# Attention outputs of a two-layer transformer block: V as the moving operand of its products instead of the stationary one

## The chip, the core and the metric

The kernel runs on one core of one Trainium2 chip. A core has five engines with queues of their own: TensorE (PE in the views, its weight loads PEld), VectorE (DVE), ScalarE (ACT), GpSimd (POOL) and SyncE (SP), which issues the transfers. TensorE reads both operands from SBUF: the stationary one (`lhsT`) is loaded first, then the moving one (`rhs`) streams through; results land in PSUM, from where VectorE or ScalarE fetch them. The metric is device time in microseconds of the whole program.

## What is computed

Two layers work on 512 latent tokens and 256 context tokens of width 1024. Each layer has attention with three groups of heads of 64 columns, then an output projection and a SwiGLU. Cut to what matters here:

```python
# A: 6 heads, 2 kv heads; keys: 512 latent + 256 context
oa = weigh(softmax(scores(qa, ka_all)), va_all)
# B: 4 heads, differential, then an RMS norm over the 64 columns of a head
p  = softmax(scores(q1, k1_all)) - lam * softmax(scores(q2, k2_all))
ob = rmsnorm(weigh(p, vb_all), g_subln) * (1 - lam_init)
# C: 6 heads, 2 kv heads; a band of up to 3 blocks of 128 keys + 256 context keys + a sink logit
p  = softmax(concat([s_loc, scores(q, kc), sink]))
oc = weigh(p_loc, v_blk) + weigh(p_ctx, vc)
ox = merge_heads(concat([oa, ob, oc]))      # then x + gate * (ox @ w_out)
```

In layer 0 the context tokens are queries as well (against context keys alone); in layer 1 only latent tokens are.

## The kernel before

All work is recorded as operations, and a planner (`Plan`) then puts them in an order by list scheduling, with a price for each (`Plan.price`) and with a choice between engines where an operation names two (`act_dve`, `dve_pool`, `plan.any`). The order of issue of each engine is fixed from then on; since all instructions are issued in one place, every row of the profile has the line 377. The sequence of the units of attention is written out in `ORDER` (letters A, B, C; small letters are steps of the modulation, P0 to P2 the projections).

A unit of A covers two heads (one of each kv head) and 256 queries as two tiles of 128; a unit of B two heads and 256 queries; a unit of C six heads and 128 queries. Layer 0 has 9 units of A, 6 of B and 6 of C, layer 1 has 6, 4 and 4. Scores are made with queries in partitions, in a PSUM tile `S` (two of them); VectorE finds the maximum of a row, ScalarE writes the exponentials to `P` and their sum to `rsum`. In A and C, `scale_rows` then multiplies P by the inverse of that sum, in place. In B, P1 - lambda P2 is formed unnormalised, and the sum goes into the later norm.

For the product with V, P is transposed on TensorE, 128 x 128 at a time, four (C: three) into one PSUM tile `T` (four of them), which is copied to an SBUF tile `pt`. In `pv_pair` the block of V (128 keys x 64 columns) is the stationary operand and `pt` (256 queries, in C 384) the moving one; the two heads of a pair write partitions 0 to 63 and 64 to 127 of `acc`, in f32. So the output comes with head columns in partitions, as the output projection wants it, and a copy to `o` ends units of A and C. `PV_RUN` puts the products of two key blocks together. In B the squares of `acc` are summed over partitions by a product with `hsel` (128 stationary columns, 2 moving ones), the inverse root is spread over partitions by a copy `rb` and a product with the identity, fetched as `rsb`, and multiplied in together with `gsub`.

The planner prices a product in f32 by the columns of its moving operand, with half the price where the output has 64 partitions:

```python
            share = {32: 4, 64: 2}.get(out.shape[0], 1)
            return max(n * 4 / 2400, 0.107) / share + 0.003
```

Of the kernel before, what the change touches and what calls it, by code (L numbers as in the profile page):

```python
# [34 lines left out]
FF_ADA = "dddd"  # L35
PV_RUN = {"A": 2, "B": 2, "C": 2}
QK_AHEAD = 238
# [12 lines left out]
SB = 32.0 ** -0.5  # L50
SLOTS = {"u": 39, "pt": 8, "s": 7, "y": 24, "rb": 2, "S": 2, "T": 4, "ropeG": 1}

# [328 lines left out]
def dit_block(  # L381
# [13 lines left out]

    pools = {tag: ctx.enter_context(tc.tile_pool(name="p" + tag, bufs=SLOTS[tag])) for tag in ("u", "pt", "s", "y", "rb")}
    cp = ctx.enter_context(tc.tile_pool(name="cp", bufs=1))
# [10 lines left out]
    def new(tag, shape, name, dt=F32):  # L408
        return plan.tile(pools[tag], [128] + list(shape), dt, tag, nm(name))
# [16 lines left out]
    def C(shape, name, dt=F32):  # L426
        return cp.tile([128] + list(shape), dt, tag=name, name=name)
# [247 lines left out]
    for l in range(2):  # L675
# [93 lines left out]
        else:  # L769
# [10 lines left out]
            act.copy(maskR, mst)  # L780
            hsel = C([2], "hsel")
            dve.memset(hsel, 0.0)
            for h in range(2):
                dve.memset(hsel[64 * h:64 * h + 64, h:h + 1], 1.0)
            ropeA = C([NX, 2, 64], "ropeA")
# [223 lines left out]

        def scale_rows(P, s):  # L1010

            plan.any([("dve", "tensor_scalar_mul", (P, P, s), {}),
                      ("act", "activation", (P, P, AF.Identity), {"scale": s})])

        def spread(rps, o, rr, n):

            rb = new("rb", [6, 64], "rb")
            dve_pool.tensor_copy(rb[:, 0:2 * n], rr.rearrange("p (h o) -> p h o", o=1).to_broadcast([128, 2 * n, 64]))
            for j in range(n):
                pe.matmul(rps[:, o + 128 * j:o + 128 * j + 128],  # L1020
                          lhsT=rb[:, 2 * j:2 * j + 2].rearrange("p h d -> p (h d)"), rhs=ident, start=True, stop=True)

        def pv_pair(acc, Ps, off, heads, kbs):

            kbs = list(kbs)
            for n0, run in pv_runs(kbs, PV_RUN["B" if heads[0] in (2, 4) else "A"]):
                pts = []
                for n in run:
                    t = PT()
                    with plan.together():  # L1030
                        for h in range(2):
                            for i in range(2):
                                pe.transpose(t[:, 256 * h + 128 * i:256 * h + 128 * i + 128],
                                             Ps[h][i][:, off + 128 * n:off + 128 * n + 128], ident)
                    pt = new("pt", [2, 256], "pt")
                    act_dve.copy(pt, t.rearrange("p (h n) -> p h n", h=2))
                    pts.append(pt)
                with plan.together():
                    for n, pt in zip(run, pts):
                        for h in range(2):  # L1040
                            pe.matmul(acc[64 * h:64 * h + 64, 0:256], lhsT=v_block(heads[h], kbs[n]), rhs=pt[:, h, :],
                                      start=(n == 0), stop=(n == len(kbs) - 1))

        def pv_runs(kbs, size):

            m = -(-len(kbs) // size)
            cuts = [len(kbs) * k // m for k in range(m + 1)]
            return [(a, range(a, b)) for a, b in zip(cuts, cuts[1:])]

# [38 lines left out]
        def attn_a():  # L1088
            stk = stack_ac("a")
            yield  # L1090
            Kx, Kc = stk[2:]
            for p, r, i0 in units(range(3)):
                k0 = 0 if r == 0 else 512
                Ps, rsum = ([], []), tiny(4)
                for j in range(2):
                    prods = []
                    for g in range(2):
                        q = q_block(stk, p, g, r, i0 + j)
                        prods.append([(q, Kx[hl][:, g], Kc[:, 2 * hl + g]) for hl in range(2)])
                    pair = score_pair(r, prods, [rsum[:, 2 * j + g:2 * j + g + 1] for g in range(2)])  # L1100
                    rr = inverse(rsum[:, 2 * j:2 * j + 2], 2)
                    for g in range(2):
                        scale_rows(pair[g][:, k0:768], rr[:, g:g + 1])
                        Ps[g].append(pair[g])
                acc = PT()
                pv_pair(acc, Ps, k0, (0, 1), range(k0 // 128, 6))
                act_dve.copy(o_cols(p, 1, r, 128 * i0, 256)[:, 0], acc[:, 0:256])
                yield

        def attn_b():  # L1110
            for p, r, i0 in units(range(2)):
# [4 lines left out]
                k0 = 0 if r == 0 else 512  # L1116
                Ps, rsum = ([], []), tiny(4)
                for j in range(2):
# [9 lines left out]
                    for hh, (P1, P2) in enumerate(pairs):  # L1128
                        dve.scalar_tensor_tensor(P1[:, k0:768], P2[:, k0:768], cf[:, hh:hh + 1], P1[:, k0:768],
                                                 op0=ALU.mult, op1=ALU.add)  # L1130
                        Ps[hh].append(P1)
                acc = PT()
                pv_pair(acc, Ps, k0, (2 + 2 * p, 3 + 2 * p), range(k0 // 128, 6))

                sq = S2([256], "sqb")
                act.activation(sq, acc[:, 0:256], AF.Square)
                for j in range(2):
                    pe.matmul(acc[:, 256 + 2 * j:258 + 2 * j], lhsT=sq[:, 128 * j:128 * j + 128], rhs=hsel, start=True, stop=True)
                w = tiny(4)
                dve.scalar_tensor_tensor(w, rsum, EPS, rsum, op0=ALU.mult, op1=ALU.mult)  # L1140
                ms = tiny(4)
                dve.scalar_tensor_tensor(ms, acc[:, 256:260], 1.0 / 64, w, op0=ALU.mult, op1=ALU.add)
                rs = tiny(4)
                pool.tensor_tensor(rs, ms, mhalf[:, 0:4], ALU.pow)
                spread(acc, 256, rs, 2)
                rsb = S2([256], "rsb")
                act_dve.copy(rsb, acc[:, 256:512])
                dve.scalar_tensor_tensor(o_cols(3 + p, 1, r, 128 * i0, 256)[:, 0], acc[:, 0:256], gsub[:, l:l + 1], rsb,
                                         op0=ALU.mult, op1=ALU.mult)
                yield  # L1150

        def attn_c():
# [4 lines left out]
            for r, i in ctx_first:  # L1157
# [3 lines left out]
                nk = 256 + nl  # L1161
                Ps, n2, rsum = ([], []), tiny(6), tiny(6)
                for j in range(3):
# [25 lines left out]
                    for g in range(2):  # L1189
                        P = new("u", [640], "P")  # L1190
                        c1 = slice(2 * j + g, 2 * j + g + 1)
                        act.activation(P[:, 0:nk], ss[g][:, 0:nk], AF.Exp, bias=n2[:, c1], accum_out=rsum[:, c1])
                        Ps[g].append(P)
                e = tiny(6)
                dve_pool.tensor_tensor(e.rearrange("p (j g) -> p j g", g=2), n2.rearrange("p (j g) -> p j g", g=2), sk, ALU.add)
                act.activation(e, e, AF.Exp)
                dve_pool.tensor_tensor(rsum, rsum, e, ALU.add)
                rr = inverse(rsum, 6)
                for j in range(3):
                    for g in range(2):  # L1200
                        scale_rows(Ps[g][j][:, 0:nk], rr[:, 2 * j + g:2 * j + g + 1])
                acc = PT()
                kbs = [4, 5] + list(range(b0, b1))
                for n0, run in pv_runs(kbs, PV_RUN["C"]):
                    pts = {}
                    for n in run:
                        for g in range(2):
                            t = PT()
                            with plan.together():
                                for j in range(3):  # L1210
                                    pe.transpose(t[:, 128 * j:128 * j + 128], Ps[g][j][:, 128 * n:128 * n + 128], ident)
                            pts[n, g] = new("pt", [384], "pt")
                            act_dve.copy(pts[n, g], t[:, 0:384])
                    with plan.together():
                        for n in run:
                            for g in range(2):
                                pe.matmul(acc[64 * g:64 * g + 64, 0:384], lhsT=v_block(6 + g, kbs[n]), rhs=pts[n, g],
                                          start=(n == 0), stop=(n == len(kbs) - 1))
                for j, n in ((0, 1), (1, 2)) if r == 0 else ((0, 3),):
                    cs = slice(128 * j, 128 * (j + n))  # L1220
                    act_dve.copy(o_cols(5 + j, n, r, 128 * i, 128), acc[:, cs].rearrange("p (k n) -> p k n", k=n))
                yield
# [382 lines left out]
```

## Time and profile before

| | |
|---|---|
| median of 3 runs | 1687.56 us (1686.57 to 1688.38) |
| profiled execution | 1688.15 us |
| its span, first to last instruction | 1686.3 us |
| mean granted TensorE clock | 0.992 |
| TensorE busy | 1636.0 us (97%) |
| VectorE busy | 1308.3 us (78%) |
| ScalarE busy | 724.6 us (43%) |

The time is that of the whole execution; the span is what the trace covers. Busy time of TensorE counts each matmul from its start to a modelled end, so neighbouring ones overlap. A product in f32 leaves two records in the trace, one for each pass, and so does its weight load.

### The profile page before, as it was taken

The page shows a single profiled execution, that of the slowest core. Times are in us where ns is not written, and L with a number is a line of the kernel's source. Part 1 is how long each engine was busy: PE and PEld are TensorE (multiplying, and loading weights), DVE is VectorE, ACT ScalarE, POOL GpSimd, SP SyncE. Part 2 cuts the span into 40 slices and gives each one's busy share as a digit, 9 for nine tenths or more (in the row PEclk, how much of TensorE's full clock was granted, in tenths as well). Part 3 has the DMA queues.
Part 4 walks back from the last instruction along what each step waited for, and adds up shares of the span by engine and source line. Part 5 has one row for each costly group of instructions (what it writes and reads, how often), then busy time and mean ns, then how long its engine had stood idle before and what let it go on. Part 6 is the DMA issues. An engine that isn't in the chain of part 4 may idle for free.

```text
span 1686.3 us, 24082 instructions
## 1 busy us (share of the span) xinstructions
PE 1636.0 (97%) x9171; PEld 1330.1 (79%) x9171; DVE 1308.3 (78%) x2238; ACT 724.6 (43%) x1441; POOL 117.9 (7%) x167
## 2 busy tenths in 40 slices
PE   7999899999999999999999999999999999999998
PEld 4787667667898888888888888777777888888886
DVE  3776889776576997987768884788886668888896
ACT  3523888774354222323211152368884542232222
POOL 0130300100000000000000001121001000000010
PEclk9999999999999999999999999999999999999999
DMA  9512231225353554443323360112023534234261
GB/s 307 204 51 75 62 97 38 82 69 144 96 191 102 175 160 152 141 147 124 103 76 87 138 188 25 38 48 55 1 55 109 150 100 126 75 101 124 75 200 50
DMA packets 153278, 182.94 MB, mean 108 GB/s; under 512 B 9316, under 2 KB 121396, under 8 KB 153164
## 3 DMA queue, kind: packets, MB, share of 16 engines
q1 hardware_dynamic: 153164, 181.42, 34.8%
q8 instruction: 72, 1.18, 0.3%
q14 instruction: 42, 0.34, 0.1%
HBM read 163.00 MB, written 9.47 MB: 102 GB/s over the span
## 4 chain that ended last, share of the span: by engine, by line
PE 82%; DVE 4%; ACT 4%; issue 1%; DMA 0%; POOL 0%; DVEq 0%; SPq 0%; POOLq 0%; ACTq 0%
PE S__1355 L377 1%; PE S__1354 L377 1%; PE S__1543 L377 1%; PE S__1765 L377 1%; PE S__1841 L377 1%; PE S__1468 L377 1%; PE S__1691 L377 1%; PE S__1908 L377 1%; PE S__2047 L377 0%; PE S__2045 L377 0%; PE S__2036 L377 0%; PE S__2034 L377 0%; PE S__1969 L377 0%; PE S__1378 L377 0%; PE S__1365 L377 0%
## 5 line engine op out<-in xcount | busy, mean ns | idle before, releaser
L377 POOL TENSOR_TENSOR t__2091<-t__2090,mhalf 128x1 f32<-128x1 f32 x1 | 0.5, 548 | 513.8 <-DVE t__2090 L377 513.8
L377 POOL TENSOR_TENSOR ws__3615<-ws__3615,gate__3614 128x512 f32<-128x512 f32 x1 | 1.3, 1298 | 285.9 <-DMA ws__3618<-in_w_ff_dram 285.9
L377 DVE TENSOR_TENSOR wl__2247<-ws__2245,wh__2246 128x1024 fp32r<-128x1024 f32 x1 | 1.2, 1227 | 10.9 <-ACT V__2170 L377 10.9
L377 ACT ACT_TABLE_LOAD x6 | 7.7, 1283 | 0.8 <-PEq L1590 0.7
L377 DVE SCALAR_TENSOR_TENSOR acc__1463<-wa__1465,cstat,acc__1463 128x1024 f32<-128x1024 f32 x1 | 1.3, 1285 | 8.1 <-ACT acc__1463 L377 8.1
L377 DVE TENSOR_TENSOR t__2200<-qr__2199,ropeB 128x128 f32<-128x128 f32 x1 | 0.3, 292 | 9.2 <-ACT qr__2199 L377 9.2
L377 ACT ACTIVATE xn__2088<-xf__2066 128x1024 f32<-128x1024 f32 x1 | 1.1, 1060 | 13.5 <-issue 13.5
L377 ACT CAST fh__1972<-sg__1929 128x384 fp32r<-128x384 f32 x1 | 0.5, 514 | 12.7 <-DVE sg__1929 L377 12.7
L377 DVE TENSOR_TENSOR sg__1356<-sg__1356,S__1355 128x768 f32<-128x768 f32 x1 | 1.0, 954 | 5.8 <-ACT acc__1374 L377 5.8
L377 ACT ACTIVATE sg__1895<-S__1884 128x768 f32<-128x768 f32 x1 | 0.8, 812 | 10.9 <-PE S__1884 L377 10.9
L377 ACT ACTIVATE sg__1958<-S__1947 128x768 f32<-128x768 f32 x1 | 0.8, 812 | 10.8 <-PE S__1947 L377 10.8
L377 PE MATMUL T__115<-wa__116,cstat 128*32 128x128 f32 x8 | 0.7, 417 | 4.9 <-DVE t__98 L377 4.9
L377 ACT ACTIVATE sg__2021<-S__2010 128x768 f32<-128x768 f32 x1 | 0.8, 812 | 10.6 <-PE S__2010 L377 10.6
L377 ACT ACTIVATE sg__2035<-S__2034 128x768 f32<-128x768 f32 x1 | 0.8, 812 | 10.4 <-PE S__2034 L377 10.4
L377 ACT CAST gh__2002<-sg__1990 128x768 fp32r<-128x768 f32 x1 | 0.8, 837 | 9.6 <-DVE sg__1990 L377 9.6
L377 ACT CAST wh__1728<-ws__1727 128x1024 fp32r<-128x1024 f32 x1 | 1.1, 1052 | 8.6 <-DMA ws__1727<-in_w_ff_dram 8.6
L377 ACT CAST wh__1577<-ws__1576 128x1024 fp32r<-128x1024 f32 x1 | 1.1, 1052 | 8.5 <-PE T__1568 L377 8.5
L377 ACT CAST wh__1502<-ws__1501 128x1024 fp32r<-128x1024 f32 x1 | 1.0, 1047 | 8.3 <-PE T__1493 L377 8.3
L377 POOL TENSOR_TENSOR ropeG<-ropeA,gqk 128x64 f32<-128x64 f32 (+1 forms) x7 | 4.1, 608 | 7.0 <-DVE gqk L377 5.7
L377 ACT CAST wh__1656<-ws__1655 128x1024 fp32r<-128x1024 f32 x1 | 1.1, 1052 | 8.1 <-DVE yw__1408 L377 8.1
L377 ACT ACTIVATE acc__1687<-wa__1686,cstat 128x1024 f32<-128x1024 f32 x1 | 1.1, 1150 | 7.8 <-PE T__1667 L377 7.8
L377 ACT ACTIVATE acc__1837<-wa__1836,cstat 128x1024 f32<-128x1024 f32 x1 | 1.1, 1150 | 7.8 <-PE T__1813 L377 7.8
(14049 smaller groups left out, 6742.8 us busy)
## 6 DMA issues: line engine op xcount, KB each, us to landing
x__83<-in_x_dram SPq DMA_DIRECT2D x1, 512.0 KB
x__84<-in_x_dram SPq DMA_DIRECT2D x1, 512.0 KB
x__131<-in_x_dram SPq DMA_DIRECT2D x1, 512.0 KB
x__136<-in_x_dram SPq DMA_DIRECT2D x1, 512.0 KB, 6.4
x__198<-in_ctx_dram SPq DMA_DIRECT2D x1, 512.0 KB
x__203<-in_ctx_dram SPq DMA_DIRECT2D x1, 512.0 KB
ws__240<-in_w_in_dram SPq DMA_DIRECT2D x1, 512.0 KB
ws__243<-in_w_in_dram SPq DMA_DIRECT2D x1, 512.0 KB
```

Source lines behind the costliest of these rows:

```text
L377: getattr(self.real[op.eng], method)(*args, **kw)
```

## The change

Products with V exchange their operands. `pv_rows` takes the rows of P one after the other (a row: one head, 128 queries), four blocks of 128 x 128 into a tile `T`, copies them to `pt`, and multiplies each with its block of V: 128 stationary columns of `pt`, 64 moving ones of V, output with queries in partitions, 64 columns of `acc` a row. P stays unscaled; `times_rows` divides (or, in B, normalises) the output with the queries in partitions, and `turn` transposes it on TensorE so that `o` has head columns in partitions as before. In B the squares are summed along the free axis on VectorE, and `hsel`, `spread`, `rb` and `rsb` go. The price formula of the planner stays as it is.

```diff
-        def scale_rows(P, s):
-            plan.any([("dve", "tensor_scalar_mul", (P, P, s), {}),
-                      ("act", "activation", (P, P, AF.Identity), {"scale": s})])
-        def spread(rps, o, rr, n):
-            rb = new("rb", [6, 64], "rb")
-            dve_pool.tensor_copy(rb[:, 0:2 * n], rr.rearrange("p (h o) -> p h o", o=1).to_broadcast([128, 2 * n, 64]))
-            for j in range(n):
-                pe.matmul(rps[:, o + 128 * j:o + 128 * j + 128],
-                          lhsT=rb[:, 2 * j:2 * j + 2].rearrange("p h d -> p (h d)"), rhs=ident, start=True, stop=True)
-        def pv_pair(acc, Ps, off, heads, kbs):
...
+        def pv_rows(acc, rows, kbs):
             kbs = list(kbs)
+            blocks = [(c, n) for c in range(len(rows)) for n in range(len(kbs))]
+            for b0 in range(0, len(blocks), 4):
+                part = blocks[b0:b0 + 4]
+                t = PT()
+                with plan.together():
+                    for b, (c, n) in enumerate(part):
+                        pe.transpose(t[:, 128 * b:128 * b + 128], rows[c][0][:, 128 * n:128 * n + 128], ident)
+                pt = new("pt", [512], "pt")
+                act_dve.copy(pt[:, 0:128 * len(part)], t[:, 0:128 * len(part)])
+                for c in sorted({c for c, _ in part}):
+                    with plan.together():
+                        for b, (c2, n) in enumerate(part):
+                            if c2 == c:
+                                pe.matmul(acc[:, 64 * c:64 * c + 64], lhsT=pt[:, 128 * b:128 * b + 128],
+                                          rhs=v_block(rows[c][1], kbs[n]), start=(n == 0), stop=(n == len(kbs) - 1))
+        def times_rows(acc, s, m):
+            ob = S2([64 * m], "ob")
+            dve.tensor_tensor(ob.rearrange("p (c d) -> p c d", d=64), acc[:, 0:64 * m].rearrange("p (c d) -> p c d", d=64),
+                              s.rearrange("p (c o) -> p c o", o=1).to_broadcast([128, m, 64]), ALU.mult)
+            return ob
+        def turn(t, o, ob, m):
+            with plan.together():
+                for b in range(m):
+                    pe.transpose(t[:, o + 128 * b:o + 128 * b + 128], ob[:, 128 * b:128 * b + 128], ident)
...
 # attn_a
-                    rr = inverse(rsum[:, 2 * j:2 * j + 2], 2)
-                    for g in range(2):
-                        scale_rows(pair[g][:, k0:768], rr[:, g:g + 1])
-                        Ps[g].append(pair[g])
+                    rows += [(pair[g][:, k0:768], g) for g in range(2)]
                 acc = PT()
-                pv_pair(acc, Ps, k0, (0, 1), range(k0 // 128, 6))
-                act_dve.copy(o_cols(p, 1, r, 128 * i0, 256)[:, 0], acc[:, 0:256])
+                pv_rows(acc, rows, range(k0 // 128, 6))
+                turn(acc, 256, times_rows(acc, inverse(rsum, 4), 4), 2)
+                act_dve.copy(o_cols(p, 1, r, 128 * i0, 256)[:, 0], acc[:, 256:512])
...
 # attn_b
-                for j in range(2):
-                    pe.matmul(acc[:, 256 + 2 * j:258 + 2 * j], lhsT=sq[:, 128 * j:128 * j + 128], rhs=hsel, start=True, stop=True)
+                dve.tensor_reduce(ss, sq.rearrange("p (c d) -> p c d", d=64), axis=AX.X, op=ALU.add)
...
-                spread(acc, 256, rs, 2)
-                rsb = S2([256], "rsb")
-                act_dve.copy(rsb, acc[:, 256:512])
-                dve.scalar_tensor_tensor(o_cols(3 + p, 1, r, 128 * i0, 256)[:, 0], acc[:, 0:256], gsub[:, l:l + 1], rsb,
-                                         op0=ALU.mult, op1=ALU.mult)
+                turn(acc, 256, times_rows(acc, rs, 4), 2)
+                scaled(o_cols(3 + p, 1, r, 128 * i0, 256)[:, 0], acc[:, 256:512], gsub[:, l:l + 1])
...
 # attn_c
-                rr = inverse(rsum, 6)
-                for j in range(3):
-                    for g in range(2):
-                        scale_rows(Ps[g][j][:, 0:nk], rr[:, 2 * j + g:2 * j + g + 1])
                 acc = PT()
...
+                pv_rows(acc, rows, [4, 5] + list(range(b0, b1)))
+                t = PT()
+                turn(t, 0, times_rows(acc, inverse(rsum, 6), 6), 3)
```

## Rows read from the trace of the kernel before

**Rows 1.** The page, part 1: busy us (share of the span) x instructions.

```profile
PE 1636.0 (97%) x9171; PEld 1330.1 (79%) x9171; DVE 1308.3 (78%) x2238; ACT 724.6 (43%) x1441; POOL 117.9 (7%) x167
```

**Rows 2.** Busy time by stretch (start:end, length; busy us and instructions of each engine).

```profile
core 0: us, PE busy (x) PEld busy (x) DVE busy (x) ACT busy (x) POOL busy (x), PEclk, DMA share, GB/s
180.00:385.00 205.00, 190.45 (x1420) 138.99 (x1418) 173.65 (x384) 163.42 (x426) 25.20 (x40) 0.98 0.27 77
400.00:480.00 80.00, 80.00 (x446) 69.66 (x445) 44.76 (x87) 34.25 (x67) 3.31 (x6) 1.00 0.43 138
1130.00:1290.00 160.00, 152.94 (x1059) 114.44 (x1058) 138.12 (x280) 130.66 (x299) 21.88 (x34) 0.98 0.21 52
1200.00:1260.00 60.00, 59.88 (x422) 44.37 (x420) 51.66 (x116) 48.87 (x112) 6.76 (x11) 1.00 0.07 20
```

**Rows 3.** TensorE's longest waits, 180:260 and 1130:1290 (total us, times, longest).

```profile
PE S__546 L377 <- ACT P__578 L377: 2.9, 1, 2.9
...
PE T__2959 L377 <- DVE P__2944 L377: 3.5, 1, 3.5
```

**Rows 4.** Timeline of TensorE in layer 0, unit of B (start us, us).

```profile
192.14 0.28 PE L377 MATMUL S__508<-bkc__348,bqx__343 128*128 128x256 f32 x1
192.35 0.65 PE L377 MATMUL T__433<-pt__435,V__214 128*64 128x256 f32 x4
...
193.27 0.60 PE L377 MATMUL T__433<-pt__439,V__215 128*64 128x256 f32 x4
193.70 0.60 PE L377 MATMUL T__433<-pt__441,V__215 128*64 128x256 f32 x4
194.23 0.50 PE L377 MATMUL S__510<-bkx__346,bqx__344 128*128 128x512 f32 x1
194.57 0.28 PE L377 MATMUL S__510<-bkc__348,bqx__344 128*128 128x256 f32 x1
194.69 0.39 PE L377 MATMUL S__514<-bkx__345,bqx__343 128*128 128x512 f32 x1
```

**Rows 5.** Timeline of TensorE in layer 0, units of C.

```profile
345.36 0.27 PE L377 MATMUL T__1077<-ident,P__1054 128*128 128x128 f32 x1
345.47 0.27 PE L377 MATMUL T__1077<-ident,P__1059 128*128 128x128 f32 x1
345.67 0.54 PE L377 MATMUL T__1062<-pt__1064,V__216 128*64 128x384 f32 x1
345.68 0.54 PE L377 MATMUL T__1062<-pt__1066,V__216 128*64 128x384 f32 x1
346.05 0.49 PE L377 MATMUL T__1062<-pt__1064,V__216 128*64 128x384 f32 x1
...
346.37 0.49 PE L377 MATMUL T__1062<-pt__1068,V__216 128*64 128x384 f32 x1
...
347.11 0.51 PE L377 MATMUL S__1125<-kc__896,qx__889 128*128 128x256 f32 x2
```

**Rows 6.** Timeline of the weight loads: sums of squares and broadcast in B.

```profile
197.47 0.53 PEld L377 LDWEIGHTS T__433<-hsel,sqb__446 128*128 128x128 f32 x4
...
200.99 0.52 PEld L377 LDWEIGHTS T__433<-ident,rb__450 128*128 128x128 f32 x4
```

**Rows 7.** View of tile T__433: duration ns min/median/max, first and last start, forms.

```profile
L377 PEld LDWEIGHTS T__433<-hsel,sqb__446 x4: 188/190/192, 197.5 to 197.8; 128*128 128x128 f32 x4
...
L377 DVE SCALAR_TENSOR_TENSOR o__452<-T__433,gsub,rsb__451 x1: 477/477/477, 202.4 to 202.4; 128x256 f32<-128x256 f32 x1
```

**Rows 8.** Timelines of VectorE and ScalarE: scalings of P, the first and others.

```profile
211.75 0.61 DVE L377 TENSOR_SCALAR P__542<-P__542,t__548 128x768 f32<-128x768 f32 x1
...
228.94 0.35 DVE L377 TENSOR_SCALAR P__665<-P__665,t__669 128x256 f32<-128x256 f32 x1
...
1251.63 0.97 ACT L377 ACTIVATE P__2873<-P__2873,t__2878 128x768 f32<-128x768 f32 x1
...
1260.50 0.61 DVE L377 TENSOR_SCALAR P__2908<-P__2908,t__2913 128x768 f32<-128x768 f32 x1
```

More of the change, by code (lines that the diff above doesn't have):

```diff
@@ L35 @@
 FF_ADA = "dddd"
-PV_RUN = {"A": 2, "B": 2, "C": 2}
 QK_AHEAD = 238
@@ L50 @@
 SB = 32.0 ** -0.5
-SLOTS = {"u": 39, "pt": 8, "s": 7, "y": 24, "rb": 2, "S": 2, "T": 4, "ropeG": 1}
+SLOTS = {"u": 39, "pt": 8, "s": 7, "y": 24, "S": 2, "T": 4, "ropeG": 1}
 class _Op:
@@ L394, in dit_block @@
     act_dve, dve_pool = plan.queue("act|dve"), plan.queue("dve|pool")
-    pools = {tag: ctx.enter_context(tc.tile_pool(name="p" + tag, bufs=SLOTS[tag])) for tag in ("u", "pt", "s", "y", "rb")}
+    pools = {tag: ctx.enter_context(tc.tile_pool(name="p" + tag, bufs=SLOTS[tag])) for tag in ("u", "pt", "s", "y")}
     cp = ctx.enter_context(tc.tile_pool(name="cp", bufs=1))
@@ L780, in dit_block @@
             act.copy(maskR, mst)
[L781 to L784, printed above, removed]
             ropeA = C([NX, 2, 64], "ropeA")
@@ L1023, in pv_pair @@
-        def pv_pair(acc, Ps, off, heads, kbs):
-            kbs = list(kbs)
[L1026 to L1029, printed above, removed]
-                    with plan.together():
[L1031 to L1048, printed above, removed]
+        def scaled(o, P, s):
+            plan.any([("dve", "tensor_scalar_mul", (o, P, s), {}), ("act", "activation", (o, P, AF.Identity), {"scale": s})])
+        def pv_rows(acc, rows, kbs):
+            kbs = list(kbs)
+            blocks = [(c, n) for c in range(len(rows)) for n in range(len(kbs))]
[8 more added lines that the diff above has]
+                for c in sorted({c for c, _ in part}):
+                    with plan.together():
+                        for b, (c2, n) in enumerate(part):
+                            if c2 == c:
+                                pe.matmul(acc[:, 64 * c:64 * c + 64], lhsT=pt[:, 128 * b:128 * b + 128],
+                                          rhs=v_block(rows[c][1], kbs[n]), start=(n == 0), stop=(n == len(kbs) - 1))
@@ L1093, in attn_a @@
                 k0 = 0 if r == 0 else 512
-                Ps, rsum = ([], []), tiny(4)
+                rows, rsum = [], tiny(4)
                 for j in range(2):
@@ L1116, in attn_b @@
                 k0 = 0 if r == 0 else 512
-                Ps, rsum = ([], []), tiny(4)
+                rows, rsum = [], tiny(4)
                 for j in range(2):
@@ L1130, in attn_b @@
                                                  op0=ALU.mult, op1=ALU.add)
-                        Ps[hh].append(P1)
+                        rows.append((P1[:, k0:768], 2 + 2 * p + hh))
                 acc = PT()
-                pv_pair(acc, Ps, k0, (2 + 2 * p, 3 + 2 * p), range(k0 // 128, 6))
-                sq = S2([256], "sqb")
+                pv_rows(acc, rows, range(k0 // 128, 6))
+                sq, ss = S2([256], "sqb"), tiny(4)
                 act.activation(sq, acc[:, 0:256], AF.Square)
-                for j in range(2):
-                    pe.matmul(acc[:, 256 + 2 * j:258 + 2 * j], lhsT=sq[:, 128 * j:128 * j + 128], rhs=hsel, start=True, stop=True)
+                dve.tensor_reduce(ss, sq.rearrange("p (c d) -> p c d", d=64), axis=AX.X, op=ALU.add)
                 w = tiny(4)
@@ L1141, in attn_b @@
                 ms = tiny(4)
-                dve.scalar_tensor_tensor(ms, acc[:, 256:260], 1.0 / 64, w, op0=ALU.mult, op1=ALU.add)
+                dve.scalar_tensor_tensor(ms, ss, 1.0 / 64, w, op0=ALU.mult, op1=ALU.add)
                 rs = tiny(4)
                 pool.tensor_tensor(rs, ms, mhalf[:, 0:4], ALU.pow)
-                spread(acc, 256, rs, 2)
-                rsb = S2([256], "rsb")
-                act_dve.copy(rsb, acc[:, 256:512])
-                dve.scalar_tensor_tensor(o_cols(3 + p, 1, r, 128 * i0, 256)[:, 0], acc[:, 0:256], gsub[:, l:l + 1], rsb,
-                                         op0=ALU.mult, op1=ALU.mult)
+                turn(acc, 256, times_rows(acc, rs, 4), 2)
+                scaled(o_cols(3 + p, 1, r, 128 * i0, 256)[:, 0], acc[:, 256:512], gsub[:, l:l + 1])
                 yield
@@ L1161, in attn_c @@
                 nk = 256 + nl
-                Ps, n2, rsum = ([], []), tiny(6), tiny(6)
+                rows, n2, rsum = [], tiny(6), tiny(6)
                 for j in range(3):
@@ L1192, in attn_c @@
                         act.activation(P[:, 0:nk], ss[g][:, 0:nk], AF.Exp, bias=n2[:, c1], accum_out=rsum[:, c1])
-                        Ps[g].append(P)
+                        rows.append((P, 6 + g))
                 e = tiny(6)
@@ L1197, in attn_c @@
                 dve_pool.tensor_tensor(rsum, rsum, e, ALU.add)
-                rr = inverse(rsum, 6)
-                for j in range(3):
-                    for g in range(2):
-                        scale_rows(Ps[g][j][:, 0:nk], rr[:, 2 * j + g:2 * j + g + 1])
                 acc = PT()
[L1203 to L1218, printed above, removed]
+                pv_rows(acc, rows, [4, 5] + list(range(b0, b1)))
+                t = PT()
+                turn(t, 0, times_rows(acc, inverse(rsum, 6), 6), 3)
                 for j, n in ((0, 1), (1, 2)) if r == 0 else ((0, 3),):
                     cs = slice(128 * j, 128 * (j + n))
-                    act_dve.copy(o_cols(5 + j, n, r, 128 * i, 128), acc[:, cs].rearrange("p (k n) -> p k n", k=n))
+                    act_dve.copy(o_cols(5 + j, n, r, 128 * i, 128), t[:, cs].rearrange("p (k n) -> p k n", k=n))
                 yield
```

## The prediction

> **What bounds the kernel now.** I read the page first. TensorE is busy for 97% of the span, VectorE for 78%, ScalarE for 43% [rows 1]. The change touches attention only, so the second view is the busy time by stretch. The attention of layer 0 lies in 180 to 385 us, that of layer 1 in 1130 to 1290 us; 400 to 480 is output projection and SwiGLU, for comparison [rows 2]. There TensorE has no pause at all (80.00 of 80). In attention it is busy 190.45 of 205 and 152.94 of 160 us, so 14.6 + 7.1 = 21.6 us of open pauses, and in 1200 to 1260 hardly any (59.88 of 60). VectorE and ScalarE are at 85% and 80% in layer 0, 86% and 82% in layer 1. So TensorE is the first bound, and the two others are close behind it. The third view is what TensorE waits for: exponentials that have not released a score tile (2.9 us), rows of P that are late (3.5 us) [rows 3]. These are the pauses into which more TensorE work could go.
>
> TensorE's busy time contains the tails of pipelined products. I therefore price every product by the distance from its start to the start of the next, not by its duration.
>
> **What the products with V cost today.** A unit of A or B takes one key block (128 keys, 2 heads, 256 queries) as two products with 64 stationary columns of V, each in two passes, four records a block. The records of the two heads start 0.01 us apart [rows 5], so they run side by side. A run of four blocks in B begins at 192.35, its last two blocks start at 193.27 and 193.70, and the next work starts at 194.23 [rows 4]: 0.43 us a block in the middle of a run. The score product at 192.14 takes 0.21 us to the next start, the same form at 194.57 takes 0.12: entering the half-array form costs 0.09. From 192.26 to 194.23 are 1.97 us = 4 x 0.43 + 0.25, so a run pays 0.25 us for going in and out. For C (384 queries a head) two pairs of records start 0.32 us apart in steady state (346.05, 346.37), so 0.64 a block; the run goes from 345.47 + 0.11 to 347.11, 1.53 us = 2 x 0.64 + 0.25 [rows 5]. The same 0.25.
>
> By the program there are 130 such blocks in A and B: layer 0 has 5 head pairs x (6 + 6 + 2) = 70 and layer 1 has 5 x 12 = 60. C has 22 + 18 = 40. The trace has 67 runs, of which the two above are shown. Sum: 130 x 0.43 + 40 x 0.64 + 67 x 0.25 = 55.9 + 25.6 + 16.8 = 98.3 us.
>
> **What they cost after.** Each block and each row of 128 queries becomes a product of its own: 128 stationary columns of P transposed, 64 moving columns of V, f32 as before. There are 130 x 4 + 40 x 6 = 760. No row of before has this form, but two rows enclose it. The sums of squares in B have 128 stationary columns and only 2 moving ones; the broadcast with rb has 128 and 128. In both, four weight loads run in 0.53 and 0.52 us, each taking 0.19 [rows 6, 7]; so from first start to last start 0.34 and 0.33 us for three steps, 0.11 us a pass, whether 2 or 128 columns move. The load of the stationary operand sets this pace. With 64 columns moving nothing lies outside these two, so I take 0.11 a pass, 0.22 a product: 760 x 0.22 = 167.2 us. That is +68.9 us on TensorE.
>
> The Trainium skill, TensorEngine Tiling (Array Packing), section When to Use Tiling, advises the opposite of this change: where the moving side has 64 columns or fewer, exchange the operands and tile the columns twofold. The rows bear it out: the kernel before does just that, and two heads share 0.43 us. By the rule alone (a factor of two lost on 81.5 us) the products would go to 163 us, by rows to 167.
>
> **The other parts.** On TensorE, the transposes of P stay as they are (0.11 each [rows 5]). New are those of the divided outputs: 2 in each of 25 units of A and B, 3 in each of 10 units of C, 80 x 0.11 = 8.8. Gone are four f32 products in each of 10 units of B (sums of squares, broadcast), 40 x 0.22 = 8.8. These cancel. TensorE's sum is +68.9.
>
> On VectorE and ScalarE the scaling of P goes: 120 instructions in the trace (79 on VectorE), of 0.35 us (256 columns) to 0.97 us (768 on ScalarE), 0.61 for the usual one [rows 8]; 120 x 0.61 = 73. In come 35 divisions that read PSUM. The nearest row is the last step of B, 0.48 us for 256 columns [rows 7]; the bounds are the 0.35 us of a scaling of 256 columns and 0.97 of one of 768 [rows 8], I take 0.5: 17 us. In B the broadcast copy, the copy rsb and the last step are replaced by a reduction and a scaled copy of much the same length, so nothing; the cover, if that is wrong, is the pause of these engines. C copies 62 times 512 columns instead of 80 times 384, nothing again. So some 55 us leave two engines, 27 each. That is no gain by itself while TensorE is the bound: it shortens the way from exponential to transpose (0.6 us a row), so it shrinks TensorE's pauses.
>
> Products of the first row can now start when this row's exponential is done; before, all rows of a unit had to be there. That too only fills pauses. After the last product come a division, two or three transposes and the copy, instead of the copy alone: about 0.5 + 0.3 + latencies, some 1 us at the end of a stage, against the 0.6 us scaling and the earlier start. I take it as nothing, with 2 us either way for two stages. No DMA is added, and SyncE's and GpSimd's queues keep their order but for the broadcast copy, which some units may have put on GpSimd.
>
> The order is made by a planner whose price for the new product is max(4 x 64 / 2400, 0.107) + 0.003 = 0.11 us, half of what the rows say. TensorE will thus fall behind the plan, and find its operands ready when it gets to them. I expect this to close pauses, not to open them.
>
> **The sum.** The profiled execution took 1688.15 us, 1686.3 of them span. +68.9 on TensorE, less the pauses that it fills. All 21.6 us of open pauses would be a plausible fill, because behind them stand waits too short for the busy time to show (a product's tail covers them), and because the shorter way through VectorE and ScalarE helps; I take 25. That gives +44: 1688 + 44 = 1732. The median of the runs shown (1687.56) is 0.6 lower, which changes nothing.
>
> **Rivals.**
> Nothing is filled: the pauses are chains of score, maximum and exponential with two score tiles, and extra work before or behind them moves them along. For it speaks that the waits are on such tiles [rows 3]. 1688 + 69 = 1757, and with 2 us for the tails 1759.
> Nearly all is filled: short pauses are as long again as the listed ones, 43 us filled, +26, so 1714; with yet shorter chains 1706. For it: the planner's too cheap price and 55 us less on the other engines. Against it: 1200 to 1260 has no pause to fill.
> The load is hidden: the new product costs what its 64 columns take, 0.11 us, as the planner thinks. Then 760 x 0.11 = 83.6, TensorE saves 15, and with lighter side engines the time is 1673 or less. It decides from a price below 98.3 / 760 = 0.129 us (0.16 with 25 us of pauses filled). Against it speak the loads 0.11 us apart with two columns moving [rows 6].
> VectorE and ScalarE are the real bound: 27 us less each makes 1661. It needs 69 us of TensorE work to vanish in pauses of which 21.6 are seen; it could only hold if the busy rows of TensorE were mostly tails.
>
> **Numbers.** Chances: forecast (1717 to 1750) 0.66; nothing filled (1750 to 1765) 0.15; nearly all filled (1695 to 1717) 0.11; load hidden 0.04; side engines 0.02; worse than all of these 0.02, if queues ordered by a wrong price stall each other. The range 1706 to 1759 reaches to the far ends of the two neighbours worked out above; it leaves out the two faster cases and the worst one. A measurement of this kernel can tell 0.2% (3.4 us). Slower 0.93, same 0.02, faster 0.05.
>
> **What would show it.** In the profile after: weight loads of the new products 0.11 us apart, 1520 of them; no scaling of P; TensorE's pauses in attention clearly below 21.6 us, VectorE and ScalarE below 80% there; both attention stages longer: layer 0 has 92 of the 170 blocks, +37 us, and two thirds of the open pauses, -17, so 205 to about 225; layer 1 +32 and -8, 160 to about 184; all other stages as before. I am wrong if the loads come closer together than 0.08 us, if TensorE's pauses grow, or if the two stages grow by less than 15 us together.

## The result, and the profile after

The changed kernel takes 1728.4 us (median of 4 runs, 1725.59 to 1729.26) against 1687.67: the ratio is 1.0239, 95% interval 1.0221 to 1.0257, so 2.4% slower. The forecast was 1732, with 1706 to 1759. The span of the profiled execution grew from 1686.3 to 1723.7, by 37.4 us.

The page, part 1, for the changed kernel (its lines have the number 376, one less than before):

```profile
PE 1687.3 (98%) x10011; PEld 1448.4 (84%) x10011; DVE 1286.9 (75%) x2153; ACT 702.1 (41%) x1400; POOL 115.4 (7%) x162
```

Weight loads went up by 118 us, VectorE and ScalarE down by 21 and 22 us [rows 1]. There are 840 more matmul records: 1520 for the products with V where 680 were, 80 new transposes, and 80 gone with the f32 products of B.

The timeline of the weight loads, a unit of C in layer 0 (start us, us):

```profile
375.30 0.53 PEld L376 LDWEIGHTS T__1095<-V__213,pt__1101 128*128 128x128 f32 x4
375.75 0.53 PEld L376 LDWEIGHTS T__1095<-V__211,pt__1103 128*128 128x128 f32 x4
376.20 0.30 PEld L376 LDWEIGHTS T__1095<-V__212,pt__1103 128*128 128x128 f32 x2
376.42 0.30 PEld L376 LDWEIGHTS T__1095<-V__213,pt__1103 128*128 128x128 f32 x2
```

Four loads take 0.45 us from start to start, 0.11 us each: the pace of the two rows that enclosed the new form [rows 6]. Added up over the trace from each record's start to the next start, the 1520 passes take 162.5 us, 0.107 a pass. The usual pass takes 0.112; the first of a run, whose weights are loaded while the work before it still streams, takes 0.058 in the median.

Busy time by stretch, attention of the two layers in the changed kernel; the third row is the middle of layer 1:

```profile
180.00:405.00 225.00, 218.00 (x1856) 200.26 (x1853) 162.55 (x334) 150.46 (x398) 25.30 (x39) 1.00 0.27 76
1150.00:1327.00 177.00, 175.21 (x1446) 168.69 (x1445) 126.55 (x246) 119.56 (x285) 18.80 (x30) 1.00 0.19 47
1220.00:1290.00 70.00, 69.82 (x584) 68.13 (x583) 47.88 (x101) 41.99 (x100) 5.32 (x10) 1.00 0.01 1
```

TensorE is idle for 7.0 us in layer 0 and 1.8 us in layer 1, 8.8 where 21.6 were [rows 2]. VectorE fell from 85 and 86% to 72 and 71%, ScalarE from 80 and 82% to 67 and 68%. The granted clock is 1.00 in both where it was 0.98.

TensorE's longest waits (total us, times, longest), layer 0 and layer 1:

```profile
PE S__575 L376 <- ACT P__509 L376: 1.7, 1, 1.7
PE T__626 L376 <- ACT bkx__611 L376: 0.9, 1, 0.9
...
PE T__2518 L376 <- ACT bkx__2492 L376: 0.7, 1, 0.7
```

They are shorter than the 2.9 and 3.5 us of [rows 3]. The other side of it is that ScalarE waits longer for TensorE (layer 0, its two longest waits for it, in the kernel before and then in the changed one):

```profile
ACT pt__1147 L377 <- PE T__1146 L377: 2.9, 1, 2.9
ACT pt__988 L377 <- PE T__987 L377: 2.1, 1, 2.1
```

```profile
ACT pt__1109 L376 <- PE T__1108 L376: 3.9, 1, 3.9
ACT o__601 L376 <- PE T__926 L376: 3.5, 1, 3.5
```

Where the time came in: the first 512-column product of the SwiGLU of layer 0 started at 475.53 before and starts 21.1 us later.

```profile
496.68 0.40 PE L376 MATMUL S__1351<-hx__1234,wh__1346 128*128 128x512 f32 x1
```

The remaining 16.3 us of the 37.4 come behind that point; layer 1's attention lies there.

### The profile page after: what moved, and what is told of

Its sections match the earlier page's. It is cut to its first block, busy times and chain, and to the rows that moved or that the text cites. A ratio compares the mean times of both kernels' runs of the same rounds, so it can differ in the third digit from the quotient of the medians.

```text
span 1723.7 us, 25650 instructions
## 1 busy us (share of the span) xinstructions
PE 1687.3 (98%) x10011; PEld 1448.4 (84%) x10011; DVE 1286.9 (75%) x2153; ACT 702.1 (41%) x1400; POOL 115.4 (7%) x162
## 4 chain that ended last, share of the span: by engine, by line
PE 86%; ACT 2%; DVE 2%; issue 1%; DMA 0%; SPq 0%; DVEq 0%; POOLq 0%; ACTq 0%
PE S__1343 L376 1%; PE S__1342 L376 1%; PE S__1531 L376 1%; PE S__1753 L376 0%; PE S__1829 L376 0%; PE S__1456 L376 0%; PE S__1896 L376 0%; PE S__1679 L376 0%; PE S__2035 L376 0%; PE S__2033 L376 0%; PE S__2024 L376 0%; PE S__2022 L376 0%; PE S__1957 L376 0%; PE S__1366 L376 0%; PE S__1353 L376 0%
```

## The experiments

Times are medians; ratios are to the kernel before on the same chip (its median there was 1688.6 to 1688.9, 1 us above the 1687.67 of the result), with 95% intervals. So a difference of 1 us to the 1728.4 of the changed kernel says nothing. "Runs" below are unbroken sequences of products with V on TensorE.

**e1_halves: the stationary side cut to 64 columns.** The same computation; only the width of a load changes, and two of them write different halves of the partitions, as the two heads did before. The planner's price for the whole product stays 0.11 us, 0.057 for each half.

```diff
-  pe.matmul(acc[:, 64 * c:64 * c + 64], lhsT=pt[:, 128 * b:128 * b + 128],
-            rhs=v_block(rows[c][1], kbs[n]), ...)
+  for h in range(0, 128, 64):
+      pe.matmul(acc[h:h + 64, 64 * c:64 * c + 64], lhsT=pt[:, 128 * b + h:128 * b + h + 64],
+                rhs=v_block(rows[c][1], kbs[n]), ...)
```

> The changed kernel with each product with V cut in two: 64 queries stationary, output in partitions 0 to 63 and 64 to 127. Theory (the load of the stationary columns sets the pace): the loads of the two halves run side by side as those of the two heads did before, so a pass takes about 0.06 us instead of 0.11 and the products some 90 us instead of 162; going in and out of the half-array form costs 0.25 us for each of perhaps 150 runs, +38. Together 34 us less on TensorE, of which the pauses give some back: 1690 to 1710, faster than the changed kernel. Rival (each pass costs 0.11 us whatever is loaded): twice the records, at best side by side, so 1728 plus the going in and out, 1740 to 1770.

Measured 1694.25 us, ratio 1.0032 (1.0020 to 1.0044): 34 us less than the changed kernel. TensorE's timeline of this kernel (eight records are two products, in halves):

```profile
186.41 0.40 PE L376 MATMUL T__429<-V__213,pt__433 128*64 128x64 f32 x8
186.64 0.40 PE L376 MATMUL T__429<-V__211,pt__433 128*64 128x64 f32 x8
186.87 0.40 PE L376 MATMUL T__429<-V__212,pt__435 128*64 128x64 f32 x8
```

Two products start every 0.23 us, 0.115 a product where the changed kernel has 0.22. In sum the products take 105.5 us instead of 162.5, although there are twice as many records. So not the number of passes and not the moving columns set the pace, but how many stationary columns are loaded one after the other; loads into the two halves go side by side (in the trace those of a pair start 6 ns apart, the next pair 52 ns later). The trace has 87 runs, not 150: the planner, which prices the change of form, put them together.

**e2_price: the planner told the true price.**

```diff
+            if out.shape[0] == 128 and n < 128:
+                return 0.222
             share = {32: 4, 64: 2}.get(out.shape[0], 1)
```

> The changed kernel, with 0.222 us instead of 0.110 as the planner's price of a product with V. Theory of the prediction (TensorE falls behind the plan and finds operands ready, so the wrong price costs nothing): within 5 us of 1728, on either side. Rival (the wrong price spoils the order of the queues): 1705 to 1720.

Measured 1741.61, ratio 1.0313 (1.0298 to 1.0328): 13 us slower than with the wrong price, outside what either theory said. The layer 1 attention by stretch in this kernel, and TensorE's longest waits there:

```profile
1150.00:1345.00 195.00, 189.33 (x1474) 177.57 (x1474) 135.71 (x269) 123.06 (x292) 14.00 (x20) 0.98 0.17 43
```

```profile
PE T__2518 L378 <- DVE bkx__2492 L378: 1.3, 1, 1.3
PE T__2508 L378 <- POOL t__2487 L378: 1.0, 1, 1.0
```

TensorE is idle for 5.7 us there where the changed kernel had 1.8, and between these two waits the granted clock fell to the lower level. The products themselves take 4.1 us more (166.6 in sum), the transposes of P 6.2. The other prices below say how far this is a rule.

**e3_scaled_p: the exchange of operands alone.**

```diff
+                    rr = inverse(rsum[:, 2 * j:2 * j + 2], 2)
+                    for g in range(2):
+                        scale_rows(pair[g][:, k0:768], rr[:, g:g + 1])
...
-                turn(acc, 256, times_rows(acc, inverse(rsum, 4), 4), 2)
+                turn(acc, 256, times_rows(acc, one4[:, 0:4], 4), 2)
...
```

> The changed kernel with P scaled before the transposes as in the kernel before; the outputs are multiplied by one in place of the division. So the exchange of operands alone, with 73 us of scaling back on VectorE and ScalarE. Theory (TensorE is the bound, its pauses are mostly filled by the longer products, the lighter engines help a little): 1730 to 1745. Rival (what was filled was due to the lighter side engines): 1750 to 1760, so the whole 65 to 69 us appear.

Measured 1738.48, ratio 1.0298 (1.0281 to 1.0315): 10 us above the changed kernel. So the 73 us of scaling are worth about 10 us of time, and the exchange alone costs about 50, not the whole 65 to 69.

**e4_no_scaling: the lighter engines alone.** The kernel before without `scale_rows`.

```diff
                     for g in range(2):
-                        scale_rows(pair[g][:, k0:768], rr[:, g:g + 1])
                         Ps[g].append(pair[g])
...
```

> The kernel before without the scaling of P in A and C (the division by the sum is left out; B is as it was). Theory (TensorE is the bound, 21.6 us of open pauses in attention): 73 us less on the two other engines bring at most a part of the pauses, 1675 to 1686. Rival (VectorE and ScalarE are the real bound in attention): 30 us or more, 1660 or less.

Measured 1683.24, ratio 0.9970 (0.9958 to 0.9981): 5 us. 73 us of work taken from VectorE and ScalarE hardly show, so those two do not bound attention.

**e5_run12, e6_run24, e11_run8, e12_run16: fewer changes of form.** As e1_halves, but the transposes and copies of several tiles come first and their products stand together in one run (8, 12, 16 or 24 blocks).

```diff
-            for b0 in range(0, len(blocks), 4):
+            for r0 in range(0, len(blocks), 12):
+                run, pts = blocks[r0:r0 + 12], []
+                for b0 in range(0, len(run), 4):
...
+                    pts.append(pt)
+                with plan.together():
+                    for b, (c, n) in enumerate(run):
+                        for h in range(0, 128, 64):
+                            q0 = 128 * (b % 4) + h
+                            pe.matmul(acc[h:h + 64, 64 * c:64 * c + 64], lhsT=pts[b // 4][:, q0:q0 + 64], ...)
```

> As e1_halves, but the products of twelve blocks stand together (three tiles of transposes first), so TensorE goes into the half-array form less often: 67 runs by the program where e1_halves had 87 in its trace. Theory (0.25 us for each run): 5 us less than the 1694 of e1_halves, 1685 to 1692, level with the kernel before. Rival (later first product, copies held longer, outweighs it): 1695 or more.

> As e5_run12 with twenty-four blocks together, a whole unit of A or B: about 40 runs. Theory (0.25 us for each run): 11 us less than e1_halves, 1681 to 1688, perhaps below the kernel before. Rival (the products of a unit wait for all its transposes and copies, and pauses open): 1690 to 1705.

> As e5_run12 with eight blocks together, so more and shorter runs (some 70 to 85 instead of 58 in the trace). Theory (0.25 us a run against the wait for the copies of a run): between e1_halves and e5_run12, 1680 to 1692. Rival (order by chance): below 1679.

> As e5_run12 with sixteen blocks together, between it (1680) and e6_run24 (1689). Theory: 1680 to 1689. Rival (order by chance): outside.

| | blocks together | runs in the trace | products, us in sum | time | ratio (interval) |
|---|---|---|---|---|---|
| e1_halves | 4 | 87 | 105.5 | 1694.25 | 1.0032 (1.0020 to 1.0044) |
| e11_run8 | 8 | 65 | 103.2 | 1679.22 | 0.9940 (0.9925 to 0.9955) |
| e5_run12 | 12 | 58 | 99.7 | 1679.66 | 0.9945 (0.9933 to 0.9958) |
| e12_run16 | 16 | 53 | 99.2 | 1680.50 | 0.9951 (0.9936 to 0.9966) |
| e6_run24 | 24 | 39 | 94.5 | 1688.88 | 1.0002 (0.9993 to 1.0011) |

With 8 to 16 blocks together the kernel is faster than the kernel before by 0.5 to 0.6% and than the changed one by 2.8%. The sum of the products falls with the number of runs, somewhat more than the 0.25 us a run say: 0.09 of it, the going in, lies ahead of the first product and so outside this sum, and 48 runs fewer from the first row to the last are 8 us at 0.16, where 11 were measured. But that is not the whole: from 4 to 8 blocks the time falls by 15 us, and 22 runs fewer are 5.5 us at 0.25. Added up from start to next start, the products take 2.3 us less, the score products 6.6 and the first form of the output projection 2.9; TensorE's idle time behind scores falls from 4.1 to 1.0 us and behind the output projection from 2.6 to 0.1. Why the planned order leaves shorter waits there is not settled. Against the kernel before, the products of e5_run12 cost more, 99.7 us and 5.9 for going into the form against 92.7 and 6.6. What it gains lies in TensorE's waits and in the clock, which falls three times in the attention of the kernel before (last section) and not in that of e5_run12; how much of the 9 us is due to each, no run separates. So e5_run12 came out better than expected (1685 to 1692), e11_run8 just below its range and e12_run16 inside it. e6_run24 lies between what its two theories said; for it the trace shows a price of waiting: attention by stretch in e5_run12 and then in e6_run24.

```profile
180.00:380.00 200.00, 190.24 (x2658) 162.26 (x2650) 163.76 (x343) 149.54 (x394) 26.10 (x38) 1.00 0.30 83
1130.00:1277.00 147.00, 142.55 (x2089) 129.17 (x2088) 118.11 (x237) 109.77 (x259) 18.92 (x27) 1.00 0.20 50
```

```profile
180.00:379.00 199.00, 188.56 (x2607) 160.93 (x2605) 161.82 (x331) 143.16 (x390) 30.38 (x44) 0.99 0.28 78
1128.00:1290.00 162.00, 150.79 (x2113) 132.98 (x2113) 125.86 (x247) 112.63 (x266) 20.74 (x33) 0.99 0.22 52
```

TensorE is idle for 14.2 us with 12 blocks and for 21.6 us with 24, most of the difference in layer 1 (4.5 and 11.2 us).

**e7_v32: half of the moving columns.**

```diff
-  pe.matmul(acc[:, 64 * c:64 * c + 64], ..., rhs=v_block(rows[c][1], kbs[n]), ...)
+  pe.matmul(acc[:, 32 * c:32 * c + 32], ..., rhs=v_block(rows[c][1], kbs[n])[:, 0:32], ...)
...
```

> The changed kernel with 32 instead of 64 moving columns of V in each product (half of the output columns are left out, the other half stands in their place). Theory (the load of 128 stationary columns sets the pace): the products stay 0.11 us a pass, and the time 1722 to 1730. Rival (the moving columns cost): 0.02 to 0.03 us a pass less, 30 to 40 us in all, 1688 to 1700.

Measured 1735.27 (1730.99 to 1745.19), ratio 1.0284 (1.0255 to 1.0312). The weight loads of the same unit of C as above, in this kernel:

```profile
375.30 0.53 PEld L376 LDWEIGHTS T__1095<-V__213,pt__1101 128*128 128x128 f32 x4
375.75 0.53 PEld L376 LDWEIGHTS T__1095<-V__211,pt__1103 128*128 128x128 f32 x4
376.20 0.30 PEld L376 LDWEIGHTS T__1095<-V__212,pt__1103 128*128 128x128 f32 x2
376.42 0.30 PEld L376 LDWEIGHTS T__1095<-V__213,pt__1103 128*128 128x128 f32 x2
```

The starts are the same to a hundredth of a microsecond; the sum of the products is 161.0 us instead of 162.5. Half of the moving columns give nothing but for the first pass of a run, which takes 0.031 us in the median instead of 0.058: there the load is out of the way. So in all other passes the load sets the pace. The time is 7 us above the changed kernel and above the range expected; the granted clock was lower, which is told at the end.

**e8_twice: twice the products.**

```diff
+  for again in range(2):
       pe.matmul(acc[:, 64 * c:64 * c + 64], lhsT=pt[:, 128 * b:128 * b + 128], rhs=v_block(rows[c][1], kbs[n]),
-                start=(n == 0), stop=(n == len(kbs) - 1))
+                start=(n == 0 and not again), stop=(n == len(kbs) - 1 and again == 1))
```

> The changed kernel with each product with V done twice into the same sum (outputs of A and C double). Theory (TensorE is the bound of attention and its pauses are nearly used up, 8.8 us open): 1520 more passes at 0.11 us come on top almost whole, 1880 to 1896. Rival (pauses or the other engines still hide a part as large as the first time, 28 us of 69): 1860 or less.

Measured 1897.14, ratio 1.1233 (1.1217 to 1.1248): 168.7 us more than the changed kernel for 1520 more passes, 0.111 us each. That is a microsecond above the range expected, which the difference between the chips alone could make: nothing was hidden any more, and the time grows by all that TensorE gets to do.

**e9_price_mid and e10_price_low: other prices.** As e2_price with 0.165 and 0.06.

> The changed kernel with 0.165 us as the planner's price of a product with V, halfway between 0.110 (1728 us) and 0.222 (1742). Theory (the higher the price, the more pauses the planned order leaves): 1730 to 1740. Rival (the order changes with any price, and the 13 us are chance): outside this, on either side.

> The changed kernel with 0.06 us as that price. Theory (a lower price closes pauses, of which 8.8 us are left): 1722 to 1728. Rival (chance): 1730 or more.

Measured 1732.60, ratio 1.0260 (1.0245 to 1.0275), and 1731.78, ratio 1.0252 (1.0235 to 1.0269). From 0.06 to 0.22 the times are 1732, 1728, 1733 and 1742. 0.165 came out in its expected range, 0.06 above its own, where the rival (chance) had it. But the intervals of these two ratios overlap that of the changed kernel (1.0221 to 1.0257), so neither is shown to differ from it. Only the 13 us of the true price stand clear, and why a true price gives the worst order is not settled.

## Why the prediction was right

**The price of a product** was the step on which all else hung, and it held: 0.11 us a pass was forecast from two rows with 2 and 128 moving columns, 0.107 on average was found. e7_v32 shows that it stays the same with 32 moving columns, e1_halves that a stationary side in two halves, loaded side by side, costs half. The sum was forecast as 167.2 us and is 162.5, 4.7 too high: a tenth of the passes, most of them the first of a run, take 0.084 us or less to the next start. The products of before, forecast as 98.3, are 92.7 in the trace by the same counting, and 6.6 more for going into the form, 99.3. So the rise is 63 us, not 68.9.

**What fills the pauses** was forecast as 25 us. The time rose by 40.7, so 23 are filled; the two profiled executions, from which the sums come, lie 37.4 apart, and by them 26 are. The size was right, the parts were not, and that is in part luck. The forecast filled all 21.6 us of idle time; 12.8 are seen to be filled (21.6 to 8.8). Some 6 us came from the clock, for which the forecast has no term: in the attention of the kernel before, TensorE worked 11.7 us at 1.2 GHz (last section), where a transpose of P takes 0.213 us to the next start instead of 0.109, and in that of the changed kernel none; half of the 11.7 is an estimate from these numbers. The remaining 7 us or so lie in waits that its busy time covers. The transposes of P, unchanged in number and form, show it: they take 82.9 us from start to start where they took 99.4, and of these 16.5 us 6.1 are idle time, about 3.5 the clock, 2.3 the going into the half-array form, and the rest such waits. Put back, the scaling costs 10 us (e3_scaled_p), so about 10 us of the fill come from the lighter engines, and the rest comes with the longer products by themselves. That nothing of a second such addition is hidden, e8_twice shows.

**The parts set to nothing**: the 80 transposes of the divided outputs take 9.7 us in the trace, the products that went took 9.0. The division of 256 columns takes 0.41 to 0.43 us, that of 384 in C 0.55 to 0.56; 0.5 was taken for all.

**By layers**, 20 and 24 us were forecast; 21 came before the SwiGLU of layer 0, 16 behind it. Layer 1 filled more than its share: 5.3 of 7.1 us of its open pauses, and the wait of 3.5 us for the last unit's rows went with the 6.8 us of low clock behind it.

**The rivals.** Nothing filled (1757): excluded by the time, and by 8.8 us of idle. Nearly all filled (1714): excluded by the time; 23 to 26 us were filled, not 43. Load hidden (1673): excluded by the loads 0.11 us apart. VectorE and ScalarE as the bound (1661): excluded by e4_no_scaling, 5 us for 73 us of their work. The rule on exchanging operands and tiling columns, cited in the prediction from the Trainium skill, TensorEngine Tiling (Array Packing), section When to Use Tiling, agrees with the runs in its second half: with columns tiled twofold, P as the stationary side costs little more than V did (99.7 us in e5_run12 against 92.7, both from start to next start), and without it the price rises to 162.5. It matters little here which operand is stationary; what the change lost was the tiling.

**One step failed in part**: that a too cheap price in the planner costs nothing because TensorE falls behind its plan. The true price is worse by 13 us, so the wrong one did no harm; but the reason given would have a lower price do better still, and at 0.06 none is seen (1.0252 against 1.0239, with overlapping intervals).

## What to carry to other kernels

Before operands are exchanged, count the stationary columns that are loaded one after the other, times the passes: with 64 moving columns in f32 the load, not the stream, was the price, and rows with fewer and with more moving columns told so beforehand. If the exchange is wanted for what it frees elsewhere (here the scaling of P, 73 us on two engines), cut the stationary side in halves that write different partitions, and let enough products stand together to pay for the change of form; that turned 2.4% slower into 0.5% faster. The 73 us of work taken from engines that are 80% busy were worth 5 us in the kernel before and 10 in the changed one, as TensorE was the bound, so price such work by the pauses of the engine that bounds.

## What the runs showed of the hardware that was not expected

The clock fell without a pause that the rows show before it. In the kernel before, it fell three times in attention, and each time TensorE had been idle for more than half of the stretch ahead. Busy time by stretch, kernel before, ahead of each fall and during it:

```profile
204.00:207.70 3.70, 1.52 (x11) 1.43 (x12) 2.92 (x4) 3.59 (x13) 1.88 (x4) 1.00 0.30 118
207.70:211.10 3.40, 3.40 (x16) 2.94 (x13) 2.48 (x7) 2.43 (x6) 0.84 (x2) 0.50 0.33 86
361.00:364.70 3.70, 1.77 (x14) 1.56 (x13) 3.53 (x10) 3.67 (x13) 0.96 (x1) 1.00 0.72 244
364.70:368.10 3.40, 3.40 (x18) 3.40 (x17) 1.62 (x5) 1.08 (x4) 0.73 (x1) 0.50 0.00 0
1269.00:1272.60 3.60, 1.74 (x15) 0.86 (x11) 3.60 (x8) 3.09 (x7) 1.37 (x2) 1.00 1.04 238
1272.60:1279.40 6.80, 4.89 (x22) 4.49 (x23) 6.80 (x9) 3.42 (x6) 0.06 (x1) 0.50 0.62 145
```

In the last of them TensorE did nothing but transposes of P from 1274.27 on, and the clock was back at the upper level at 1279.5. The changed kernel has shorter pauses and no fall in attention. In e7_v32 there are three in layer 0, two of them (at 377.8 and 398.3) behind a stretch without any pause. The same view of e7_v32, ahead of the first of these two and during it:

```profile
374.00:377.80 3.80, 3.80 (x36) 3.80 (x35) 1.12 (x4) 1.66 (x4) 0.00 (x0) 1.00 0.11 38
377.80:381.20 3.40, 3.40 (x18) 3.40 (x16) 2.03 (x3) 0.00 (x0) 0.00 (x0) 0.51 0.65 191
```

And the changed kernel in the same two stretches; in the first it has the same loads at the same starts, and 64 moving columns instead of 32:

```profile
374.00:377.80 3.80, 3.80 (x36) 3.80 (x35) 1.11 (x4) 1.66 (x4) 0.00 (x0) 1.00 0.11 38
377.80:381.20 3.40, 3.40 (x31) 3.33 (x29) 2.58 (x6) 0.40 (x1) 0.00 (x0) 1.00 0.65 192
```

It stays at 2.4 GHz and does 31 matmuls where e7_v32 does 18 at 1.2 GHz. So a stretch in which the rows show no gap doesn't guarantee the upper level; the ends of the matmuls in them are modelled, so a full row need not be full work. The four executions of e7_v32 had a mean granted clock of 0.992, 0.991, 0.989 and 0.984, and times of 1731, 1734, 1736 and 1745 us in that order; the 7 us above the changed kernel go with that, though no run isolates them.
